# Half of an up product moved from the end of the scan stage to the front of the kernel

## The chip, the core and the metric

The kernel runs on one core of a Trainium2 chip. The metric is the device time of one execution in microseconds. A core has TensorE for matrix products (results go to PSUM, eight banks of 2 KB per partition), VectorE, ScalarE and GpSimd for work on tiles of 128 partitions in SBUF, and SyncE, whose queue issues most of the transfers here. The profile calls them PE (PEld for its weight loads), DVE, ACT, POOL and SP (SPq). Each engine takes its instructions in the order of its own list.

## What is computed

One step of a small encoder with 1024 prompt rows, 32 sample rows and two layers, of width 1024. Layer 0 has a scan mixer (SSD), layer 1 attention. After each mixer a gated product of a second input p is added:

```python
def ple(h, p, up_w, norm_w, gate_w):
    g = jax.nn.sigmoid((rmsnorm(h, norm_w) @ gate_w).astype(F32)).astype(h.dtype)
    return (p @ up_w).astype(h.dtype) * g
...
        hn_p = rmsnorm(hp, ln_w[i])
...
        hp = hp + yp
        hp = hp + ple(hp, p_prompt[i], ple_up_w[i], ple_norm_w[i], ple_gate_w[i])
```

The product `p @ up_w` (256 x 1024 weights) needs neither the mixer nor h: it can be computed at any time before layer 0's gate.

## The kernel before

All products are made of three matmuls on operands that are split into a high and a low part (`wh`, `wl` of a weight; `hh`, `hl` of an activation): high x high, high x low, low x high. `load_weight` issues the load of a weight on SP's queue, makes the high part on ScalarE (or on VectorE, where `eng_h` says so) and the low part, a subtraction, on GpSimd. `gemm` issues the three matmuls for each block of 128 rows.

The scan stage, `phase_ssd`, holds columns of x in three tiles (384, 384 and 292 columns). At its start ten matmuls on a tile of ones (`busy`) run while x arrives. For each tile x is loaded in four quarters; ScalarE, VectorE and GpSimd square it (`sq`), VectorE adds pairs, TensorE sums them over the partitions (`psn`, four matmuls), ScalarE makes `r`, the factor of the norm, with Ln and Exp, VectorE multiplies (`hf`), ScalarE rounds (`hh`) and GpSimd, or VectorE for blocks 1 and 5, subtracts (`hl`). The first products, a 32-column one for dt and block 0 of the input projection, follow on TensorE. Then eight groups of heads are projected, convolved and scanned.

The up product of layer 0, `up_product`, is a generator. Up to its first `yield` it loads the two halves of p transposed (`upr`) and splits them (`upx`). Then, for each of eight output blocks m, 18 matmuls fill three PSUM tiles (`mm`, 352 columns each), ScalarE evacuates them into `upe`, and the block is stored to DRAM (`u_d`). With `nb=4` one weight load and split serves four blocks. In the kernel before all of it, 144 matmuls, stands at the end of the scan stage: the last group's gate and norm (`gate`, `finish`) are written between its loads and its matmuls, so that both run side by side. `finish` walks y in three pieces: squares on ScalarE (`ysq`), a sum on GpSimd, high part on ScalarE (`ysh`), low part on GpSimd (`ysl`), two matmuls that sum over partitions (`psy`), a copy on ScalarE (`yr`); then Ln and Exp of the whole, and VectorE writes y, which is stored. The output projection, `phase_out`, reads y back (`yraw`, split into `yhl`) and multiplies it by `outW` into `pso`: for three output blocks first the 8 older blocks of y, 144 matmuls, then the rest.

The order of the instructions on each engine is set when the kernel is built, by a scheduler with a timeline of its own; a code line that moves can so move instructions of other lines. Pools set limits: `mm` has three PSUM buffers, weights have two buffers of each part, `cx` and `raw`, in which the up product's tiles lie, six each.

Of the kernel before, what the change touches and what calls it, by code (L numbers as in the profile page):

```python
# [10 lines left out]
F32 = mybir.dt.float32  # L11
F32R = mybir.dt.float32r
# [5 lines left out]
P = 128  # L18

T1 = 1060  # L20
RAWB = 6
# [3 lines left out]
T = 1056  # L25
# [147 lines left out]
def bc_last(ap, n):  # L173
    return ap.unsqueeze(len(ap.shape)).to_broadcast(list(ap.shape) + [n])
# [6 lines left out]
def rsqrt(nc, c, out, ps, scale, eps):  # L181
    nc.scalar.activation(out, ps, AF.Ln, bias=eps, scale=scale)
    nc.scalar.activation(out, out, AF.Exp, scale=-0.5)
# [8 lines left out]
def load_weight(c, src, nk, m, scale=None, eng_h=None, wp=None):  # L192
    nc = c.nc
    wp = wp or c.wp
    raw = wp.tile([P, nk, m], F32, tag="wraw", name="wraw")
    nc.sync.dma_start(raw, src)
    if scale is not None:
        nc.gpsimd.tensor_tensor(raw, raw, bc_last(scale, m), op=ALU.mult)
    wh = wp.tile([P, nk, m], F32R, tag="wh", name="wh", bufs=c.whb)
    wl = wp.tile([P, nk, m], F32R, tag="wl", name="wl", bufs=c.whb)  # L200
    if eng_h:
        eng_h.tensor_copy(wh, raw)
    else:
        nc.scalar.activation(wh, raw, AF.Copy)  # L204
    nc.gpsimd.tensor_tensor(wl, raw, wh.bitcast(F32), op=ALU.subtract)  # L205
    return wh, wl


def gemm(c, ps, w, acts, sl, m=P, first=True, last=True):
    wh, wl = w  # L210
    n = len(acts)
    for k, (ah, al) in enumerate(acts):
        a, b = ah[:, sl], al[:, sl]
        for i, (ww, aa) in enumerate(((wh, a), (wh, b), (wl, a))):
            c.nc.tensor.matmul(ps, ww[:, k, :m], aa, start=first and k == 0 and i == 0, stop=last and k == n - 1 and i == 2)  # L215


def split(c, h, l, x, eng_h=None, eng_l=None):
    nc = c.nc
    (eng_h or (lambda o, i: nc.scalar.activation(o, i, AF.Copy)))(h, x)  # L220
    (eng_l or nc.vector).tensor_tensor(l, x, h.bitcast(F32), op=ALU.subtract)  # L221


def pvc(c, name, i=0, n=1, rows=P):
    o, _ = PV[name]
    return c.pv[:rows, o + i : o + i + n]


def up_product(c, i, piece, raw, tiles, ps_tile, evac, nb=1):

    nc, I = c.nc, c.I
    o, n = piece
    acts = []
    for k in range(2):
        x = raw()[:, :n]
        nc.sync.dma_start(x, I[f"pT{i}"][:, k, o : o + n])
        h, l = tiles()[:, :n], tiles()[:, :n]
        split(c, h, l, x)
        acts.append((h, l))
    yield  # L240
    na = -(-n // 512)
    w_ = n // na
    for m in range(8):
        b = m % nb
        if b == 0:
            ws = load_weight(c, I[f"upW{i}"][m // 4][:, 2 * (m % 4) : 2 * (m % 4 + nb)], 2 * nb, P)
        w = [x[:, 2 * b : 2 * b + 2] for x in ws]
        u = evac()
        for a in range(na):
            ps = ps_tile()  # L250
            gemm(c, ps[:, :w_], w, acts, slice(w_ * a, w_ * a + w_))
            nc.scalar.activation(u[:, w_ * a : w_ * a + w_], ps[:, :w_], AF.Copy)  # L252
        c.store(c.u_d[i][m][:, o : o + n], u[:, :n])
        yield
# [8 lines left out]
def phase_ssd(c, ctx):  # L263
    nc, tc, I, O = c.nc, c.tc, c.I, c.O
# [3 lines left out]
    mm = es.enter_context(tc.tile_pool(name="ps_mm", bufs=3, space=bass.MemoryType.PSUM))  # L268
# [8 lines left out]
    kp = es.enter_context(tc.tile_pool(name="keep", bufs=1))  # L277
    with tc.tile_pool(name="xin", bufs=2, side="right") as xp:
        def busy(x, k):

            ps = pc.tile([P, 512], F32, tag="trx", name="busy")
            for _ in range(k):
                nc.tensor.matmul(ps[:, : x.shape[-1]], c.ones, x, start=True, stop=True)

        busy(c.ones, 10)
        for j, (o, n) in enumerate(TILES1):
            xt = xp.tile([P, 8, n], F32, tag=f"xt{j}", name=f"xt{j}", bufs=1)
            for q in range(4):
                nc.sync.dma_start(xt[:, 2 * q : 2 * q + 2, :], I["xT"][:, 2 * q : 2 * q + 2, o : o + n])
            if j == 0:  # L290
                c.load_constants()
                early = [load_weight(c, I["dtW"], 8, 32, eng_h=nc.vector), load_weight(c, I["inW"][0], 8, P, eng_h=nc.vector)]
            ps = pc.tile([P, 512], F32, tag="st", name=f"psn{j}")
            for q in range(4):
                sq = [xp.tile([P, n], F32, tag="sq", name=f"sq{j}_{q}", bufs=6) for _ in range(2)]
                nc.scalar.activation(sq[0], xt[:, 2 * q], AF.Square)
                if j and q % 2:
                    nc.gpsimd.tensor_tensor(sq[1], xt[:, 2 * q + 1], xt[:, 2 * q + 1], op=ALU.mult)
                elif j == 0:
                    nc.vector.tensor_tensor(sq[1], xt[:, 2 * q + 1], xt[:, 2 * q + 1], op=ALU.mult)  # L300
                else:
                    nc.scalar.activation(sq[1], xt[:, 2 * q + 1], AF.Square)
                nc.vector.tensor_tensor(sq[0], sq[0], sq[1], op=ALU.add)
                nc.tensor.matmul(ps[:, :n], c.ones, sq[0], start=q == 0, stop=q == 3)
            r = xp.tile([P, n], F32, tag="r", name=f"r{j}")
            rsqrt(nc, c, r, ps[:, :n], 1.0 / 1024, c.eps)
            if j == 0:
                busy(r, 2)
            for k in range(8):
                hf = xp.tile([P, n], F32, tag="hf", name=f"hf{j}_{k}", bufs=3)  # L310
                nc.vector.scalar_tensor_tensor(hf, xt[:, k], pvc(c, "lnw0", k), r, op0=ALU.mult, op1=ALU.mult)
                hh, hl = hn[j][0][k], hn[j][1][k]
                nc.scalar.activation(hh, hf, AF.Copy)
                (nc.vector if k % 4 == 1 else nc.gpsimd).tensor_tensor(hl, hf, hh.bitcast(F32), op=ALU.subtract)

    def mblock(*blocks, ws=None):

        ws = ws or [load_weight(c, wsrc, 8, m) for wsrc, m, _ in blocks]
        for j, (o, n) in enumerate(TILES1):
            for w, (_, m, evac) in zip(ws, blocks):  # L320
                ps = mm.tile([P, 512], F32, tag="mm", name="mm")
                acts = list(zip(hn[j][0], hn[j][1]))
                gemm(c, ps[:m, :n], w, acts, slice(0, n), m)
                evac(j, o, n, ps[:m, :n])
# [92 lines left out]
    def gate(g, b, S):  # L417

        z = raw_block(I["inW"][6 * g + 4 + b])[:, 3:]
        th = kp.tile([P, 3 + T1], F32, tag="raw", name="zs", bufs=RAWB)[:, 3:]  # L420
        sigmoid2(nc, z, th, z)
        yb = S["y"][:, b]
        nc.gpsimd.tensor_tensor(yb, yb, z, op=ALU.mult)
# [120 lines left out]
    def bc_blocks(g):  # L544
        Ss[g]["B"] = conv_block(I["inW"][6 * g], 16 + g, None if g else first)
        Ss[g]["C"] = conv_block(I["inW"][6 * g + 1], 24 + g)

    def x_block(g, b):
        Ss[g].setdefault("x", []).append(conv_block(I["inW"][6 * g + 2 + b], 2 * g + b))
# [5 lines left out]
    for g in range(G):  # L555
        scan_group(g, Ss[g])
        if g + 1 < G:
            bc_blocks(g + 1)
        if g:
            gate(g - 1, 0, Ss[g - 1])  # L560
            gate(g - 1, 1, Ss[g - 1])
        if g + 1 < G:
            x_block(g + 1, 0)
        else:
            gate(g, 0, Ss[g])
        if g:
            finish(g - 1, Ss[g - 1])
        if g + 1 < G:
            x_block(g + 1, 1)
        else:  # L570
            up = up_product(c, 0, (0, T), lambda: kp.tile([P, T1], F32, tag="cx", name="upr", bufs=6),
                            lambda: kp.tile([P, 3 + T1], F32R, tag="raw", name="upx", bufs=RAWB),
                            lambda: mm.tile([P, 512], F32, tag="mm", name="mm"),
                            lambda: kp.tile([P, T1], F32, tag="cx", name="upe", bufs=6), 4)
            next(up)
            gate(g, 1, Ss[g])
            finish(g, Ss[g])
# [546 lines left out]
def run(*gens):  # L1124
    for g in gens:
        for _ in g:
            pass
# [177 lines left out]
def build(tc, nc, I, O, dbg=None, ngroups=8, upto=9):  # L1305
# [4 lines left out]
    with ctx:  # L1310
# [40 lines left out]

        ln_exp()
        phase_ssd(c, ctx)
        if upto < 2:
            return
# [130 lines left out]
```

## Time and profile before

| | us |
|---|---|
| median of 3 runs (2016.47 to 2018.35) | 2016.96 |
| the profiled execution | 2012.76 |
| its span, first to last instruction | 2011.0 |
| TensorE busy | 1932.2 |
| VectorE busy | 1282.6 |
| ScalarE busy | 1023.8 |
| GpSimd busy | 971.6 |

The span is what the profile's rows cover; the execution's time holds 1.8 us around it. The profiled execution is a run of its own, beside the three that were timed. Starts are counted from the first instruction. A row with an idle time in brackets names who ended the wait.

### The profile page before, as it was taken

How to read it: one execution, taken by the hardware profiler on the slowest of the kernel's cores; microseconds unless marked ns; L12 is line 12 of the kernel's file. 1: busy time of each engine (PE TensorE's matmuls, PEld its weight loads, DVE VectorE, ACT ScalarE, POOL GpSimd, SP SyncE). 2: the span in 40 equal slices, each digit the busy share in tenths (PEclk: the TensorE clock that was granted, in tenths of full speed). 3: DMA queues.
4: the chain of work that ended last, by engine and by line, in shares of the span. 5: the costliest groups of instructions: out<-in, count | busy, mean ns of one | idle time of the engine just before them, and what ended most of it. 6: DMA issues, size and time to landing. Idle time of an engine off the chain costs nothing. (4 is left out here: it accounts for less than half of the span.)

```text
span 2011.0 us, 32658 instructions
## 1 busy us (share of the span) xinstructions
PE 1932.2 (96%) x12871; PEld 1773.9 (88%) x12871; DVE 1282.6 (64%) x1601; ACT 1023.8 (51%) x1757; POOL 971.6 (48%) x813
## 2 busy tenths in 40 slices
PE   7989999999999999999998999999899999999999
PEld 5989899999999998999998999777777777779999
DVE  7898575858576675443267534274688787986544
ACT  4444444453545457334243432587687877754331
POOL 5433334344444444454678443122545453645772
PEclk8999999999999999999999999999999999999999
DMA  3143333334242446544333312533512221315432
GB/s 130 53 94 90 85 91 77 86 99 99 73 104 64 104 109 214 178 140 161 100 114 119 94 55 85 164 105 96 118 47 72 54 66 36 108 59 193 127 126 74
DMA packets 110730, 204.27 MB, mean 102 GB/s; under 512 B 18224, under 2 KB 60720, under 8 KB 110448
## 3 DMA queue, kind: packets, MB, share of 16 engines
q1 hardware_dynamic: 105472, 193.17, 32.5%
q0 software_dynamic: 2800, 6.91, 1.9%
q8 instruction: 101, 1.65, 0.3%
q10 hardware_dynamic: 2304, 2.10, 0.3%
q14 instruction: 53, 0.43, 0.1%
HBM read 156.81 MB, written 38.83 MB: 97 GB/s over the span
## 5 line engine op out<-in xcount | busy, mean ns | idle before, releaser
L205 POOL TENSOR_TENSOR wl<-wraw,wh 128x1024 fp32r<-128x1024 f32 (+2 forms) x185 | 374.1, 2024 | 413.7 <-ACT wh L204 371.5
L215 PE MATMUL mm<-hh,wh 128*128 128x384 f32 (+3 forms) x1176 | 386.0, 329 | 4.7 <-ACT raw L330 4.5
L215 PE MATMUL mm<-hl,wh 128*128 128x384 f32 (+3 forms) x1176 | 387.6, 330 | 0.0
L215 PE MATMUL mm<-hh,wl 128*128 128x384 f32 (+3 forms) x1176 | 385.4, 328 | 0.0
L204 ACT ACTIVATE wh<-wraw 128x1024 fp32r<-128x1024 f32 (+3 forms) x183 | 159.1, 869 | 280.8 <-PE pso L215 117.8
L215 PE MATMUL pso<-yhl,wh 128*128 128x264 f32 x1536 | 283.5, 285 | 5.6 <-ACT upe L252 2.9
L215 PEld LDWEIGHTS pso<-yhl,wh 128*128 128x128 f32 x1536 | 239.8, 189 | 7.0 <-DVE yhl L221 3.8
L215 PEld LDWEIGHTS mm<-hh,wh 128*128 128x128 f32 (+1 forms) x1176 | 220.3, 187 | 8.9 <-ACT raw L330 5.2
L215 PEld LDWEIGHTS mm<-hl,wh 128*128 128x128 f32 (+1 forms) x1176 | 220.8, 188 | 4.6 <-issue 2.4
L215 PEld LDWEIGHTS mm<-hh,wl 128*128 128x128 f32 (+1 forms) x1176 | 220.5, 187 | 4.2 <-issue 1.9
L215 PE MATMUL pso<-yhl,wl 128*128 128x264 f32 x768 | 219.3, 286 | 4.1 <-POOL wl L205 4.1
L413 DVE SCALAR_TENSOR_TENSOR cx<-raw,pv,cx 128x1060 f32<-128x1060 f32 x96 | 132.6, 1381 | 88.3 <-ACT cx L411 87.6
L215 PE MATMUL psi<-yhl,wh 128*128 128x264 f32 (+1 forms) x896 | 167.0, 287 | 3.9 <-ACT yhl L220 3.8
L215 PEld LDWEIGHTS pso<-yhl,wl 128*128 128x128 f32 x768 | 145.2, 189 | 4.7 <-POOL wl L205 4.7
L488 POOL TENSOR_TENSOR hm<-hT,cd_all 128x256 f32<-128x256 f32 x64 | 67.6, 1057 | 165.5 <-DVE hT L490 100.7
L215 PE MATMUL pg<-hH,wl 128*128 128x264 f32 x512 | 145.9, 285 | 0.7 <-POOL wl L205 0.7
L215 PE MATMUL pg<-hH,wh 128*128 128x264 f32 x512 | 145.9, 285 | 0.0
L215 PE MATMUL pg<-hL,wh 128*128 128x264 f32 x512 | 145.7, 285 | 0.0
L215 PEld LDWEIGHTS psi<-yhl,wh 128*128 128x128 f32 (+1 forms) x896 | 138.2, 185 | 5.6 <-ACT yhl L220 4.0
L1238 PE MATMUL st<-qk 128*128 128x512 f32 (+2 forms) x576 | 139.8, 358 | 0.9 <-ACT pf L1244 0.5
L215 PE MATMUL psi<-yhl,wl 128*128 128x264 f32 (+1 forms) x448 | 129.6, 289 | 1.1 <-POOL wl L205 1.1
L1259 POOL TENSOR_TENSOR pl<-pf,ph 128x512 fp32r<-128x512 f32 x64 | 81.3, 1271 | 102.1 <-DVE ph L1258 93.5
(517 smaller groups left out, 4579.0 us busy)
## 6 DMA issues: line engine op xcount, KB each, us to landing
wraw<-in_inW SPq DMA_DIRECT2D x48, 512.0 KB, 3.5
ex<-acs_d SPq DMA_DIRECT2D x32, 512.0 KB, 5.2
wraw<-in_outW SPq DMA_DIRECT2D x32, 512.0 KB, 3.6
yraw<-y_d SPq DMA_DIRECT2D x32, 264.0 KB, 4.6
u<-u_d SPq DMA_DIRECT2D x32, 264.0 KB, 2.8
eb<-ea_d SPq DMA_DIRECT2D x64, 128.0 KB, 4.0
y_d<-y SPq DMA_DIRECT2D x16, 512.0 KB, 2.9
wraw<-in_gateW SPq DMA_DIRECT2D x16, 512.0 KB, 3.6
```

The lines of the kernel that those rows point to most:

```text
L204: nc.scalar.activation(wh, raw, AF.Copy)
L205: nc.gpsimd.tensor_tensor(wl, raw, wh.bitcast(F32), op=ALU.subtract)
L215: c.nc.tensor.matmul(ps, ww[:, k, :m], aa, start=first and k == 0 and i == 0, stop=last and k == n - 1 and i == 2)
L413: nc.vector.scalar_tensor_tensor(xh, raw[:, k : k + T1], pvc(c, "cw", 4 * b + k), xh, op0=ALU.mult, op1=ALU.add)
L488: nc.gpsimd.tensor_tensor(hm.rearrange("p (h q) -> p h q", q=64), hT.rearrange("p (h q) -> p h q", q=64), bc_last(cd_all[:, hs, ch], 64), ...
L1238: nc.tensor.matmul(ps[:, :n], a_[:, ks], b_[:, q], start=t == 0, stop=t == 2)
L1259: (nc.gpsimd if idx in L_POOL else nc.vector).tensor_tensor(pl[:, :n], pf[:, :n], ph[:, :n].bitcast(F32), op=ALU.subtract)
```

## The change

`up_product` can now do a part of the blocks (`ms`) with a weight that is handed in. Blocks 0 to 3 are done at the front of the scan stage: their weight and p are loaded and split ahead of x (`next(up)`), the weight's high part on VectorE, and the matmuls are written behind the norm of x's first tile (`run(up)`). The loads and splits of the first projection weights (`early`) move from ahead of that norm to behind it. Blocks 4 to 7 stay at the end of the stage, and p is loaded and split there a second time.

```diff
-def up_product(c, i, piece, raw, tiles, ps_tile, evac, nb=1):
+def up_product(c, i, piece, raw, tiles, ps_tile, evac, nb=1, ms=range(8), weights=None):
...
-    for m in range(8):
+    for m in ms:
         b = m % nb
         if b == 0:
-            ws = load_weight(c, I[f"upW{i}"][m // 4][:, 2 * (m % 4) : 2 * (m % 4 + nb)], 2 * nb, P)
+            ws = weights or load_weight(c, I[f"upW{i}"][m // 4][:, 2 * (m % 4) : 2 * (m % 4 + nb)], 2 * nb, P)
...
+        def up0(ms, **kw):
+            return up_product(c, 0, (0, T), lambda: kp.tile([P, T1], F32, tag="cx", name="upr", bufs=6),
+                              lambda: kp.tile([P, 3 + T1], F32R, tag="raw", name="upx", bufs=RAWB),
+                              lambda: mm.tile([P, 512], F32, tag="mm", name="mm"),
+                              lambda: kp.tile([P, T1], F32, tag="cx", name="upe", bufs=6), 4, ms, **kw)
+
         busy(c.ones, 10)
+
+        up = up0(range(4), weights=load_weight(c, I["upW0"][0], 8, P, eng_h=nc.vector))
+        next(up)
         for j, (o, n) in enumerate(TILES1):
...
             if j == 0:
                 c.load_constants()
-                early = [load_weight(c, I["dtW"], 8, 32, eng_h=nc.vector), load_weight(c, I["inW"][0], 8, P, eng_h=nc.vector)]
...
+            if j == 0:
+                early = [load_weight(c, I["dtW"], 8, 32, eng_h=nc.vector), load_weight(c, I["inW"][0], 8, P, eng_h=nc.vector)]
+                run(up)
...
-            up = up_product(c, 0, (0, T), lambda: kp.tile([P, T1], F32, tag="cx", name="upr", bufs=6),
-                            lambda: kp.tile([P, 3 + T1], F32R, tag="raw", name="upx", bufs=RAWB),
-                            lambda: mm.tile([P, 512], F32, tag="mm", name="mm"),
-                            lambda: kp.tile([P, T1], F32, tag="cx", name="upe", bufs=6), 4)
+            up = up0(range(4, 8))
             next(up)
```

How this moves instructions is seen at three places. TensorE at the front, before: the sums of the first tile follow the ten matmuls on ones, and the first projection (`mm` from `hh`) follows `r`.

```order
L283 MATMUL busy_186<-ones_115 128x128 x10
L304 MATMUL psn0_219<-sq0_0_220,ones_115 128x384
L304 MATMUL psn0_219<-sq0_1_226,ones_115 128x384
L304 MATMUL psn0_219<-sq0_2_232,ones_115 128x384
L304 MATMUL psn0_219<-sq0_3_238,ones_115 128x384
L283 MATMUL busy_247<-r0_244,ones_115 128x384 x2
L215 MATMUL mm_424<-hh0_0_132,wh_209 32x384
```

In the changed kernel, from the third to the last of these sums (`upx` 205 and 206 are high and low part of p's first half, 211 and 212 of its second):

```order
L312 MATMUL psn0_225<-sq0_2_238,ones_115 128x384
L215 MATMUL mm_353<-upx_205,wh_199 128x352
L215 MATMUL mm_353<-upx_206,wh_199 128x352
L215 MATMUL mm_353<-upx_205,wl_200 128x352
L215 MATMUL mm_353<-upx_211,wh_199 128x352
L215 MATMUL mm_353<-upx_212,wh_199 128x352
L215 MATMUL mm_353<-upx_211,wl_200 128x352
L312 MATMUL psn0_225<-sq0_3_244,ones_115 128x384
```

Ahead of these rows stand 36 up matmuls, with the first two sums among them: 42 of the 72 stand ahead of the first tile's last sum, 18 more ahead of the second tile's sums, and the last 12 ahead of the first projection.

ScalarE at the same place, before, from Ln and Exp of `r` to the first two rounded blocks:

```order
L182 ACTIVATE r0_244<-psn0_219,eps_120 128x384
L183 ACTIVATE r0_244<-r0_244 128x384
L296 ACTIVATE sq1_0_288<-xt1_282 128x384
L302 ACTIVATE sq1_0_289<-xt1_282 128x384
L313 ACTIVATE hh0_0_132<-hf0_0_250 128x384
L313 ACTIVATE hh0_1_134<-hf0_1_254 128x384
```

In the changed kernel:

```order
L182 ACTIVATE r0_250<-psn0_225,eps_120 128x384
L304 ACTIVATE sq1_2_422<-xt1_404 128x384
L310 ACTIVATE sq1_2_423<-xt1_404 128x384
L183 ACTIVATE r0_250<-r0_250 128x384
L252 ACTIVATE upe_352<-mm_361 128x352
L304 ACTIVATE sq1_3_428<-xt1_404 128x384
L252 ACTIVATE upe_352<-mm_369 128x352
L304 ACTIVATE sq2_0_475<-xt2_469 128x292
L321 ACTIVATE hh0_0_132<-hf0_0_256 128x384
L252 ACTIVATE upe_378<-mm_379 128x352
L321 ACTIVATE hh0_1_134<-hf0_1_260 128x384
```

Two squares of the second tile now stand between Ln and Exp, and evacuations of the up product and more squares ahead of `hh`. On VectorE 36 rows stand from the first `hf` to the last where there were 38: three sums of the second tile's squares stand ahead of them now, and the cast of block 0's weight among them.

TensorE at the end of the scan stage, before, from the low part of the last norm piece (`psy` with `ysl`) on; two more tiles of the up product stand between it and the output projection (`pso`):

```order
L260 MATMUL psy_7528<-ysl_7525,ones_r_117 128x292
L215 MATMUL mm_7743<-upx_7399,wh_7652 128x352
L215 MATMUL mm_7743<-upx_7400,wh_7652 128x352
L215 MATMUL mm_7743<-upx_7399,wl_7653 128x352
L215 MATMUL mm_7743<-upx_7405,wh_7652 128x352
L215 MATMUL mm_7743<-upx_7406,wh_7652 128x352
L215 MATMUL mm_7743<-upx_7405,wl_7653 128x352
```

In the changed kernel, from the end of the last up tile on:

```order
L215 MATMUL mm_7763<-upx_7527,wl_7665 128x352
L260 MATMUL psy_7628<-ysl_7625,ones_r_117 128x384
L259 MATMUL psy_7639<-ysh_7635,ones_r_117 128x384
L260 MATMUL psy_7639<-ysl_7636,ones_r_117 128x384
L259 MATMUL psy_7650<-ysh_7646,ones_r_117 128x292
L260 MATMUL psy_7650<-ysl_7647,ones_r_117 128x292
L215 MATMUL pso_7893<-yhl_7798,wh_7898 128x264
```

The last two norm pieces, which lay among up matmuls, now follow one another directly, and the output projection stands right behind them.

## Rows read from the trace of the kernel before

**Rows 1.** The page: TensorE's busy time, its share of the span and its matmuls.

```profile
PE 1932.2 (96%) x12871; PEld 1773.9 (88%) x12871; DVE 1282.6 (64%) x1601; ACT 1023.8 (51%) x1757; POOL 971.6 (48%) x813
```

**Rows 2.** Busy time by stretches: the stretch, its length, each engine's busy time and instructions, TensorE's granted clock, the DMA engines' share and GB/s.

```profile
5.00:10.00 5.00, 3.98 (x12) 1.49 (x10) 3.79 (x10) 1.86 (x4) 0.72 (x1) 1.00 1.06 382
...
20.00:25.00 5.00, 5.00 (x15) 3.48 (x15) 5.00 (x8) 2.17 (x5) 2.46 (x3) 0.50 0.00 0
...
785.00:790.00 5.00, 4.84 (x29) 4.70 (x30) 5.00 (x5) 5.00 (x13) 3.08 (x2) 1.00 0.80 311
```

**Rows 3.** Timeline of the first norm, 0 to 50 us: start, duration, engine, line, operation; in brackets the idle time ahead and who ended it. L304 is psn, L182 and L183 are Ln and Exp, L311 is hf.

```profile
4.05 0.56 DVE L300 TENSOR_TENSOR sq<-xt 128x384 f32<-128x384 f32 x1 [2.78 <-DMA xt<-in_xT]
...
7.45 0.55 DVE L300 TENSOR_TENSOR sq<-xt 128x384 f32<-128x384 f32 x1
...
8.76 0.91 PE L304 MATMUL psn<-sq,ones 128*128 128x384 f32 x2 [0.25 <-DVE sq L303]
...
9.71 0.58 ACT L182 ACTIVATE r<-psn,eps 128x384 f32<-128x384 f32 x1 [1.80 <-PE psn L304]
...
10.21 0.69 DVE L202 CAST wh<-wraw 128x1024 fp32r<-128x1024 f32 x1 [1.01 <-DMA wraw<-in_inW]
10.32 0.52 ACT L183 ACTIVATE r<-r 128x384 f32<-128x384 f32 x1
10.88 4.34 DVE L311 SCALAR_TENSOR_TENSOR hf<-xt,pv,r 128x384 f32<-128x384 f32 x3
...
11.26 0.52 ACT L296 ACTIVATE sq<-xt 128x384 f32<-128x384 f32 x1 [0.42 <-DMA xt<-in_xT]
...
15.15 1.35 DVE L303 TENSOR_TENSOR sq<-sq,sq 128x384 f32<-128x384 f32 x1
...
18.34 2.45 DVE L303 TENSOR_TENSOR sq<-sq,sq 128x384 f32<-128x384 f32 x2
...
26.56 0.84 DVE L303 TENSOR_TENSOR sq<-sq,sq 128x292 f32<-128x292 f32 x2 [1.04 <-ACT sq L302]
28.96 2.92 DVE L311 SCALAR_TENSOR_TENSOR hf<-xt,pv,r 128x384 f32<-128x384 f32 x3 [1.57 <-ACT r L183]
...
45.80 0.51 DVE L311 SCALAR_TENSOR_TENSOR hf<-xt,pv,r 128x292 f32<-128x292 f32 x1
```

**Rows 4.** Timeline of TensorE in the same stretch: a matmul in 20 to 25 us, the end of the second tile and the start of the third.

```profile
22.30 0.52 PE L215 MATMUL mm<-hh,wl 128*32 128x384 f32 x1
22.62 0.52 PE L215 MATMUL mm<-hh,wh 128*32 128x384 f32 x1
...
42.62 0.34 PE L215 MATMUL mm<-hh,wl 128*128 128x384 f32 x1
47.22 0.45 PE L215 MATMUL mm<-hh,wh 128*32 128x292 f32 x1 [4.26 <-ACT raw L330]
...
53.01 0.29 PE L215 MATMUL mm<-hh,wh 128*128 128x292 f32 x1
53.14 0.30 PE L215 MATMUL mm<-hl,wh 128*128 128x292 f32 x1
```

**Rows 5.** The up product at the end of the scan stage: timeline of its splits and of three matmuls, and the answer on the tile upe (least, median and longest duration in ns, first and last start).

```profile
765.38 1.09 ACT L220 ACTIVATE upx<-upr 128x1056 fp32r<-128x1056 f32 x1
...
770.15 1.24 DVE L221 TENSOR_TENSOR upx<-upr,upx 128x1056 fp32r<-128x1056 f32 x1
...
783.22 0.49 PE L215 MATMUL mm<-upx,wh 128*128 128x352 f32 x2
783.54 0.33 PE L215 MATMUL mm<-upx,wl 128*128 128x352 f32 x1
...
L252 ACT ACTIVATE upe<-mm x24: 443/462/534, 776.3 to 805.6; 128x352 f32<-128x352 f32 x24
```

**Rows 6.** Timeline from the first up matmul to the output projection, 774 to 812 us. L527 is ysq, L221 ysl, L534 the copy yr, L182 and L183 Ln and Exp with the table loads ahead of them.

```profile
774.68 0.32 PE L215 MATMUL mm<-upx,wh 128*128 128x352 f32 x1
...
781.17 0.59 PE L215 MATMUL mm<-upx,wh 128*128 128x352 f32 x2 [2.12 <-ACT upe L252]
...
794.76 1.02 POOL L221 TENSOR_TENSOR ysl<-ysq,ysh 128x384 fp32r<-128x384 f32 x1
...
796.42 0.69 ACT L527 ACTIVATE ysq<-y 128x584 f32<-128x584 f32 x1
...
798.57 0.82 POOL L221 TENSOR_TENSOR ysl<-ysq,ysh 128x292 fp32r<-128x292 f32 x1 [0.56 <-ACT ysh L220]
...
801.47 0.41 ACT L534 ACTIVATE yr<-psy 128x292 f32<-128x292 f32 x1
801.89 1.28 ACT L182 ACT_TABLE_LOAD   x1
803.19 1.18 ACT L182 ACTIVATE yr<-yr,eps 128x1060 f32<-128x1060 f32 x1
...
806.07 0.51 PE L215 MATMUL pso<-yhl,wh 128*128 128x264 f32 x2 [2.93 <-ACT upe L252]
...
807.33 1.09 ACT L183 ACTIVATE yr<-yr 128x1060 f32<-128x1060 f32 x1
...
811.35 0.41 PE L215 MATMUL pso<-yhl,wh 128*128 128x264 f32 x2
...
811.72 0.41 PE L215 MATMUL pso<-yhl,wh 128*128 128x264 f32 x2
```

## Prediction

> **What bounds the kernel now.** I read the page's shares of busy time first: TensorE is busy 96% of the span [rows 1], so a microsecond is won only where TensorE waits or runs slowly. I then went to the two places that the change touches. At the **front** the table by stretches shows a core that fills its DMA engines, at 382 GB/s, and a TensorE at clock 0.50 in 20 to 25 us [rows 2]. The timeline of the first norm names the chain: quarters of x land, VectorE squares and adds, TensorE sums four psn matmuls, ScalarE makes r, and from 10.88 us VectorE works through the products hf until 46.31 us [rows 3]. TensorE follows it: it has nothing after 42.62 us, waits 4.26 us for an evacuation that stands behind the last hh on ScalarE, and starts the third tile at 47.22 us with 24 matmuls that take 5.8 us to 53.01, 0.24 us each, where the next one takes 0.13 [rows 4]. So the front ends when VectorE's last hf is done; TensorE has room there. At the **seam** between the scan and the output projection, TensorE runs the 144 up matmuls at 0.163 us each (three in 0.49) [rows 5], while ScalarE, busy all of 785 to 790 us [rows 2], and GpSimd walk the last group's norm (ysq, ysh, ysl, three times) beside 24 evacuations. The last evacuation stands behind a table load, and the first pso matmul waits 2.93 us for it, until 806.07 us [rows 6].
>
> **The seam, part by part.** *Taken away:* 72 matmuls, 72 x 0.163 = 11.7 us of TensorE; 12 evacuations of 0.46 us [rows 5], 5.5 us of ScalarE; four stores and one weight load. The operand pT is still loaded and split there, so that cost stays. *What comes last instead:* up to the twelfth evacuation both orders read alike, so the up matmuls that are left end near 790.6 us. Behind them TensorE's queue now holds the psy pairs of the second and third piece, and only then pso: pso can't go before the norm has given its third piece. That chain moves little. GpSimd's second ysl ends at 795.78 us as before, since the weight split ahead of it stays; then the third ysq starts 0.6 us sooner, at 795.8 instead of 796.42, no longer behind two evacuations. From there to the end of the third ysl took 2.97 us [rows 6], so it is done at 798.8, and two psy matmuls later, at 799.2 us, pso begins: **6.9 us sooner**, not 11.7. *What that costs:* TensorE waits about 8.4 us there instead of 2.93. After the 2.93 us, the first ten triples of pso took 5.28 us, to 811.35, where the next triple takes 0.37 [rows 6]: 1.6 us lost. In 20 to 25 us the engine was busy throughout and stayed low all five [rows 2], so a longer wait may lose 2.5 us: **0.9 us back**. *What could be late next:* the last two blocks of y. Behind the third psy stand an evacuation, two table loads, Ln and Exp, 0.41 + 1.28 + 1.18 + 1.28 + 1.09 = 5.2 us, so Exp ends at 804.4 instead of 808.42 [rows 6], 4.0 us sooner; VectorE's y and their stores follow. They are needed only after 144 pso matmuls and most of the next 48, some 20 us behind the first; I put 0.1 us. The seam gives **-5.9 us**; bounds -2.9 (only the wait for the evacuation goes) and -11.7 (all the matmuls' time).
>
> **The front, part by part.** *Transfers:* 512 KB of weights and 2 x 528 KB of pT now stand first on SP's queue, ahead of x: 1.61 MB, 4.2 us at 382 GB/s [rows 2]. So x lands from 8.2 to 11.7 us instead of 4.05 to 7.45 [rows 3]. *Splits:* two of 1.09 us on ScalarE, two of 1.24 on VectorE [rows 5] and a weight split on GpSimd. pT lands at about 5.8 and 7.2 us and the splits lie in the wait for x, but for the second low part, which stands behind x's first square on VectorE and ends near 10.4 us. *Matmuls:* the last psn matmul now stands behind 42 up matmuls. The first 18 need that low part and end near 11.5; the other 24 take 3.9 us and the four psn between them, 0.91 us each when alone [rows 3] and about half of that in a stream, some 1.8. That makes 17.2 us, where it was 9.67. Then r: Ln 0.58, two squares of x's second tile that now stand between (1.04), Exp 0.52 [rows 3] and two hops, 19.6. **VectorE's first hf starts 8.7 us later**. *What VectorE saves behind it:* three sums of the second tile's squares now stand ahead of hf, 1.35 + 2.45 = 3.8 us; block 0's weight cast, 0.69 at 10.21 us [rows 3], stands behind it now: -3.1. Its two waits of 1.04 and 1.57 us [rows 3] came from the second tile's squares and their psn, which are now done ahead: -2.6. *New:* on ScalarE five evacuations stand among the hh; the first three, with two squares, hold hh 1, for which VectorE's hl 1 waits some 1.5 us, the others 0.5: +2.0. Sum 8.7 - 3.1 - 2.6 + 2.0 = **+5.0 us** on the end of the norm and on the third tile's start. Bounds: +0.5 (only the transfers delay, 4.2 + 2.0 - 5.7) and +10.7 (no saving on VectorE comes); I take the middle, since each term has its own row. The stores of u wait at SP behind all of x, with 0 GB/s in 20 to 25 us [rows 2]: nothing. GpSimd's subtract for the second weight now falls among the hl pieces, as it fell among the hf before: nothing, up to 2.4 us at worst, in the bound. TensorE has 16 instead of 9 matmuls to do after the last hl piece of the second tile, which shortens its 4.26 us wait to about 3.1; behind 2.93 us at 806 us matmuls ran slowly too [rows 6], so I leave the 24 x 0.11 = 2.6 us of slow matmuls in [rows 4]; as a bound they go.
>
> In 20 to 25 us TensorE ran its real work at 0.50, the 1.2 GHz level [rows 2]; the up matmuls will keep it busy ahead of that work. The Trainium skill (TensorE: Matmul & The Clock Gate, "What's actually happening") says that low is the resting state and that work lifts it. By that rule alone the five slow microseconds would give back 2.5 us more and the sum would be 3.4 us below the median; by the rows they give nothing beyond VectorE's two waits, since TensorE still stood idle for 4.26 us at the end of the front [rows 4].
>
> **Between the two** the orders read alike; further on a few rows of the attention part trade places, which I price at nothing, within 0.5 us.
>
> **Sum.** +5.0 - 5.9 = -0.9 us. The profiled execution took 2012.76 us, 1.76 more than its span, and lies 4.2 us below the median of the runs, 2016.96; its terms carry over as differences: 2016.96 - 0.9 = **2016.0 us**. A measurement of this kernel can tell about 0.2%, 4.0 us, from no change; this is inside it.
>
> **Rivals.** (1) *The front hides nearly all of it, faster.* If the 42 matmuls start as soon as the first pT is split, at 7.2 us, they end with their psn near 14.3 instead of 17.2, when x has just landed: -2.9; and if the clock stays up behind TensorE's shorter wait, the 2.6 us of slow matmuls go too. -0.9 - 5.5 = -6.4: 2010.6. For it: behind a wait of 2.12 us at 781 us three matmuls soon took 0.49 again [rows 5, 6]; against it, the second low part behind x's first square. (2) *The clock falls ahead of the up matmuls, slower.* The ten warming matmuls end near 5.5 us and the operands come between 7 and 10.4. If the clock falls in that wait, the 42 matmuls in front of the norm run at 0.32 us, as one of 384 columns did at 22.30 [rows 4], instead of 0.163: 42 x 0.157 = 6.6 us on a chain that everything follows, 2022.6. It turns the sign from 6 slow matmuls on (0.9 / 0.157) and passes 0.2% from 31. Against it: the clock stood at 1.00 in 5 to 10 us with work in bits [rows 2]. (3) *The seam gives no more than its old wait.* If the norm's last piece comes when it came before, pso starts little sooner and with a colder clock: -2.9 instead of -5.9, 2019.1. For it, the norm's chain is almost unchanged; against it, the twelve evacuations that leave ScalarE.
>
> **How the numbers follow.** Forecast 0.40, (1) 0.30, (2) 0.19, (3) 0.11. The predicted time is the forecast's, 2016.0. The forecast's own range, with half of each bound, is 2012 to 2020. The range of 8 in 10 goes to just beyond (1) and to (2): 2009.5 to 2022.5. Faster by over 0.2%: nearly all of (1) and a little of the forecast, 0.32. Slower by over 0.2%: (2) and a little of the others, 0.22. Within: 0.46.
>
> **What would show it.** In the changed kernel: the first hf on VectorE near 19.6 us, the last near 51, and the third tile's start on TensorE near 52 (right for the front); under 49 speaks for (1), over 56 for (2), with a granted clock under 1 between 10 and 20 us. At the seam, counted from the first up matmul there: first psy of the last pair 24 us on and pso 24.5 us on instead of 31.4, with a granted clock near 0.5 behind it. Wrong would be: a pso that waits for yhl or for weights after 144 matmuls, or a move of the time that neither place holds.

## The result and the profile after

The changed kernel takes 2021.07 us (median of 20 executions, 2015.63 to 2025.97) beside 2015.74 us for the kernel before (20 executions, 2009.43 to 2019.67). The ratio is 1.0029 with a 95% interval of 1.0019 to 1.0039: it is slower, by 3.8 to 7.9 us. The forecast was 0.9 us faster. The time lies in the range, but the forecast had the sign wrong.

The profiled execution took 2022.79 us with a span of 2021.0; the one of before took 2012.76 with 2011.0. These two differ by 10 us, more than the medians do, so single traces are compared below place by place, and each place is held against the other traces of the study.

**The front.** First the table by stretches (as [rows 2], with the stretch behind the seam added): length, each engine's busy time, TensorE's granted clock, DMA share, GB/s.

```profile
5.00:10.00 5.00, 3.13 (x11) 2.38 (x10) 3.29 (x4) 3.14 (x4) 2.39 (x2) 1.00 1.04 385
20.00:25.00 5.00, 5.00 (x26) 4.07 (x25) 2.80 (x6) 4.82 (x14) 1.74 (x2) 1.00 1.05 410
...
785.00:790.00 5.00, 3.38 (x22) 3.10 (x20) 1.62 (x1) 4.97 (x8) 3.51 (x2) 1.00 0.88 268
...
805.00:810.00 5.00, 2.96 (x9) 2.24 (x10) 1.27 (x2) 2.63 (x5) 1.93 (x3) 0.50 0.98 379
```

Then the timeline of the changed kernel from the warm-up to the first transpose of the scan (answers to [rows 3, 4]; L312 is psn, L182 and L183 are Ln and Exp, L319 is hf):

```profile
1.06 4.64 PE L283 MATMUL busy<-ones 128*128 128x128 f32 x20 [1.06 <-DVE eps L1355]
6.94 1.25 PE L215 MATMUL mm<-upx,wh 128*128 128x352 f32 x3 [1.25 <-ACT upx L220]
8.81 0.66 PE L215 MATMUL mm<-upx,wh 128*128 128x352 f32 x1 [0.62 <-DVE upx L221]
9.27 0.49 PE L215 MATMUL mm<-upx,wl 128*128 128x352 f32 x1
9.56 0.49 PE L215 MATMUL mm<-upx,wh 128*128 128x352 f32 x1
...
13.37 1.12 PE L312 MATMUL psn<-sq,ones 128*128 128x384 f32 x2
...
14.65 0.32 PE L215 MATMUL mm<-upx,wl 128*128 128x352 f32 x1
14.81 0.48 PE L215 MATMUL mm<-upx,wh 128*128 128x352 f32 x2
...
19.48 0.81 PE L312 MATMUL psn<-sq,ones 128*128 128x384 f32 x2
...
20.33 0.58 ACT L182 ACTIVATE r<-psn,eps 128x384 f32<-128x384 f32 x1 [0.18 <-PE psn L312]
...
22.24 1.67 DVE L319 SCALAR_TENSOR_TENSOR hf<-xt,pv,r 128x384 f32<-128x384 f32 x3
...
54.02 0.51 DVE L319 SCALAR_TENSOR_TENSOR hf<-xt,pv,r 128x292 f32<-128x292 f32 x1
...
55.44 0.45 PE L215 MATMUL mm<-hh,wh 128*32 128x292 f32 x1 [3.78 <-ACT raw L341]
...
108.11 0.30 PE L461 MATMUL trx<-cst,cx 128*128 128x128 f32 x1 [1.98 <-DVE cx L189]
```

Look at the starts, not at the durations. From 9.27 to 9.56 us one up matmul of 352 columns takes 0.29 us, and all 18 ahead of the first psn go at that pace; from 14.65 to 14.81 one takes 0.16. Per column 0.29 us is the pace of the 384 columns at 22.30 us of before, where the granted clock stood at 0.50 [rows 2, 4]: the 1.2 GHz level. The column of the granted clock reads 1.00 in 5 to 10 us and doesn't show it. The warm-up's rows do: its 20 passes (two to a matmul) take 4.64 us, 0.23 each, where eight more of them in e4 below take 1.29, 0.16 each. In this trace the level had not risen by the time the up matmuls came. The last psn ends at 20.29 us (17.2 forecast, 9.67 before), the first hf starts at 22.24 (19.6; 10.88), the last hf ends at 54.53 (51.3; 46.31), and the third tile starts at 55.44 (52; 47.22 [rows 3, 4]). The first transpose of the scan stands at 108.11; before it stood at 101.13.

**The seam**, from the first up matmul there to the output projection (as [rows 6]):

```profile
784.08 0.32 PE L215 MATMUL mm<-upx,wh 128*128 128x352 f32 x1
...
790.58 0.59 PE L215 MATMUL mm<-upx,wh 128*128 128x352 f32 x2 [2.19 <-ACT upe L252]
...
802.79 0.69 PE L259 MATMUL psy<-ysh,ones_r 128*128 128x384 f32 x1 [2.65 <-ACT ysh L220]
805.14 0.69 PE L260 MATMUL psy<-ysl,ones_r 128*128 128x384 f32 x1 [1.65 <-POOL ysl L221]
807.46 0.61 PE L259 MATMUL psy<-ysh,ones_r 128*128 128x292 f32 x1 [1.63 <-ACT ysh L220]
808.34 0.61 PE L260 MATMUL psy<-ysl,ones_r 128*128 128x292 f32 x1 [0.27 <-POOL ysl L221]
808.74 0.64 PE L215 MATMUL pso<-yhl,wh 128*128 128x264 f32 x2
```

Here the forecast holds. From the first up matmul to pso are 24.66 us (24.5 forecast, 31.39 before [rows 6]); the psy pairs now wait four times, 6.2 us in all, for the norm of the last group, and the clock is 0.50 in 805 to 810 us, where the last pair and the first pso matmuls stand.

**Far behind both**, in the second output product at 1820 to 1850 us, VectorE's queue has another order. The timeline of VectorE there, first of the kernel before (L221 yhl: subtractions for the coming half; L664 hf: evacuation of pso):

```profile
1824.77 1.38 DVE L221 TENSOR_TENSOR yhl<-yraw,yhl 128x528 fp32r<-128x528 f32 x2 [7.72 <-ACT yhl L220]
1827.52 2.08 DVE L221 TENSOR_TENSOR yhl<-yraw,yhl 128x528 fp32r<-128x528 f32 x3 [1.37 <-ACT yhl L220]
1829.63 0.71 DVE L664 TENSOR_TENSOR hf<-pso,xres 128x528 f32<-128x528 f32 x1
```

and then of the changed kernel, where L672 is hf, with the matmul that waits for it:

```profile
1833.57 3.38 DVE L221 TENSOR_TENSOR yhl<-yraw,yhl 128x528 fp32r<-128x528 f32 x5 [8.36 <-ACT yhl L220]
1838.16 0.71 DVE L221 TENSOR_TENSOR yhl<-yraw,yhl 128x528 fp32r<-128x528 f32 x1 [1.21 <-ACT yhl L220]
1840.28 1.42 DVE L221 TENSOR_TENSOR yhl<-yraw,yhl 128x528 fp32r<-128x528 f32 x2 [1.41 <-ACT yhl L220]
1841.73 1.32 DVE L672 TENSOR_TENSOR hf<-pso,xres 128x528 f32<-128x528 f32 x2
...
1842.58 0.48 PE L215 MATMUL pso<-yhl,wh 128*128 128x264 f32 x2 [0.77 <-DVE hf L672]
```

Before, the first evacuation stood behind five subtractions; now it stands behind eight, and TensorE waits for it. From the first pso matmul there to the first pg matmul are 97.5 us; before they were 96.0.

### The profile page after: what moved, and what is told of

It is laid out like the page before. It is cut to its first block, busy times and chain, and to the rows that moved or that the text cites. A ratio compares the mean times of both kernels' runs of the same rounds, so it can differ in the third digit from the quotient of the medians.

```text
span 2021.0 us, 32673 instructions
## 1 busy us (share of the span) xinstructions
PE 1936.9 (96%) x12871; PEld 1776.7 (88%) x12871; DVE 1295.0 (64%) x1604; ACT 1024.7 (51%) x1758; POOL 967.6 (48%) x813
## 5 line engine op out<-in xcount | busy, mean ns | idle before, releaser
L204 ACT ACTIVATE wh<-wraw 128x1024 fp32r<-128x1024 f32 (+2 forms) x182 | 157.8, 868 | 271.1 <-PE pso L215 110.5
```

## The experiments

**Theory 1**: the front costs what its trace shows and the seam gives what its trace shows. **Theory 2** (rival): the front's cost is the transfers alone. **Theory 3** (rival): the loss arises elsewhere, through the other order of the work behind the seam.

**e1, the front alone** (against the changed kernel):

```diff
-            up = up0(range(4, 8))
+            up = up0(range(8))
```

> The front of the changed kernel with the seam of the kernel before: blocks 0 to 3 are made at the front and all eight blocks again at the end of the scan stage, so four blocks are made twice. Theory 1 (the whole loss is the norm's delay at the front, 7.0 us in the two traces at 60 us, and the seam gives its 6.7 us back): 7 us over the kernel before, pso 31 us behind the first up matmul of the seam. Theory 2 (the transfers ahead of x are what delays the norm): the same here. Theory 3 (front and seam cancel at +0.3, and some 5 us more are lost behind the seam, through the other order of the work in the attention part and behind it): 12 us over before if that comes with the front, 7 if it comes with the shorter seam.

Measured 2025.89 us beside 2014.76, ratio 1.0056 (1.0039 to 1.0072): 7.9 to 14.5 us over, middle 11.3. The first transpose comes at 108.56, pso 31.6 us behind the first up matmul. Its table by stretches shows the slow up matmuls in the granted clock, as the changed kernel's does not:

```profile
10.00:15.00 5.00, 5.00 (x17) 4.39 (x17) 2.84 (x7) 2.33 (x5) 0.00 (x0) 0.53 1.08 375
```

More than the front's 7 us is lost, so theory 1 alone falls short; the 12 us of theory 3 lie in the interval.

**e2, the seam alone.** Blocks 0 to 3 are left out; the results of blocks 4 to 7 are stored twice.

```diff
+        if i == 0:
+            c.store(c.u_d[i][m - 4][:, o : o + n], u[:, :n])
...
-        up = up0(range(4), weights=load_weight(c, I["upW0"][0], 8, P, eng_h=nc.vector))
-        next(up)
...
                 c.load_constants()
+                early = [load_weight(c, I["dtW"], 8, 32, eng_h=nc.vector), load_weight(c, I["inW"][0], 8, P, eng_h=nc.vector)]
...
-            if j == 0:
-                early = [load_weight(c, I["dtW"], 8, 32, eng_h=nc.vector), load_weight(c, I["inW"][0], 8, P, eng_h=nc.vector)]
-                run(up)
```

> The seam of the changed kernel with the front of the kernel before: blocks 0 to 3 of the up product are left out, and the results of blocks 4 to 7 are stored a second time in their place. Theories 1 and 2: the seam gives its 6.7 us (31.4 less 24.7 from the first up matmul to pso), so 6 to 7 us under before. Theory 3: the loss behind the seam eats most of it, 0 to 2 us under before, and the trace shows the stretch from pso to the end some 5 to 7 us longer than before's 1204.9 us.

Measured 2011.66 us beside 2014.76, ratio 0.9985 (0.9970 to 0.9999): 0.2 to 6.0 us under, middle 3.0. Its trace has the whole gain (24.55 us from the first up matmul, 774.62, to pso):

```profile
797.88 0.61 PE L261 MATMUL psy<-ysh,ones_r 128*128 128x292 f32 x1 [1.39 <-ACT ysh L220]
798.76 0.61 PE L262 MATMUL psy<-ysl,ones_r 128*128 128x292 f32 x1 [0.27 <-POOL ysl L221]
799.17 0.64 PE L215 MATMUL pso<-yhl,wh 128*128 128x264 f32 x2
```

but its second output product takes 97.2 us. Timed, the gain lies between the 6 to 7 us of theories 1 and 2 and the 0 to 2 of theory 3. The sign that theory 3 named is not there: from pso to the end this trace takes 1204.6 us, where before took 1204.9. e1 and e2 together (+11.3 - 3.0 = +8.3) agree with the change within their intervals.

**e3, transfers and splits alone:**

```diff
-                run(up)
...
-            up = up0(range(4, 8))
+            up = up0(range(8))
```

> The transfers and the splits of the up product's operands stand at the front as in the changed kernel, but no up matmul does; all eight blocks are made at the end, with loads of their own, so the front's operands are not used. Theory 1 (the up matmuls ahead of the norm's sums make the delay, the transfers only part of it): first hf at 16 to 18 us instead of 10.9 and 22.2, 2 to 4 us over before. Theory 2 (the transfers alone do it): first hf at 20 to 22 us, 7 us over before. Theory 3 says nothing of the front; 5 us more than either if its loss comes with the splits and loads.

Measured 2020.76 us beside 2014.76, ratio 1.0027 (1.0014 to 1.0040). The trace:

```profile
10.84 5.55 PE L312 MATMUL psn<-sq,ones 128*128 128x384 f32 x8 [5.15 <-DVE sq L311]
...
17.59 5.08 DVE L319 SCALAR_TENSOR_TENSOR hf<-xt,pv,r 128x384 f32<-128x384 f32 x3 [0.20 <-ACT r L183]
...
50.67 0.45 PE L215 MATMUL mm<-hh,wh 128*32 128x292 f32 x1 [3.80 <-ACT raw L340]
```

The first hf is 6.7 us late, as theory 1 had it (17.59, short of theory 2's 20 to 22), the third tile only 3.5, and the first transpose (103.30) 2.2. Theory 2 falls: transfers and splits together make less than half of the delay of the third tile, which is 8.2 us in the changed kernel. The measured 2.8 to 8.1 us are again more than the front shows.

**e5, the loads behind the first tile's x** (the two lines that make `up` move into `if j == 0`, behind `c.load_constants()`):

> The changed kernel with the loads of upW and pT put behind the x of the first norm tile and the constants; on TensorE the first tile's four sums then stand ahead of all up matmuls, and most of these ahead of the second tile's sums. Theory 1: the first hf comes at 11 to 12 us as before, the up matmuls run while VectorE makes the first tile, a part of the 7.0 us stays (1 to 4 us, by the evacuations among the casts of ScalarE and the later x tiles), the seam keeps its 6.7: 3 to 6 us under the kernel before. Theory 2: the same or a little less, as x of tiles 1 and 2 still waits for 1.6 MB (4.2 us at 382 GB/s): 1 to 3 us under before. Theory 3: 5 us more than these, 0 to 2 us over before.

Measured 2023.94 us beside 2014.76, ratio 1.0052 (1.0032 to 1.0072). This fell for every theory: the first hf does come at 11.40 us, but the third tile starts at 58.57.

```profile
14.93 2.05 DVE L221 TENSOR_TENSOR upx<-upr,upx 128x1056 fp32r<-128x1056 f32 x1
...
20.49 2.05 DVE L221 TENSOR_TENSOR upx<-upr,upx 128x1056 fp32r<-128x1056 f32 x1
...
22.59 0.66 PE L215 MATMUL mm<-upx,wh 128*128 128x352 f32 x1 [2.55 <-DVE upx L221]
...
31.59 0.57 ACT L182 ACTIVATE r<-psn,eps 128x384 f32<-128x384 f32 x1
...
39.10 0.36 PE L215 MATMUL mm<-hh,wh 128*32 128x384 f32 x1 [0.59 <-ACT upe L252]
```

The two splits now stand among the products hf, at 2.05 us instead of 1.24 [rows 5]; the evacuations stand among ScalarE's casts, and the second tile's r comes at 31.59. The last hf ends at 52.22, 5.9 us later than before. That is only half of the third tile's 11.4 us; the rest stands in TensorE's own list. All 72 up matmuls stand there ahead of the first projection. They wait for their operands, and it starts at 39.10, where before it started at 12.66:

```profile
12.66 0.54 PE L215 MATMUL mm<-hh,wh 128*32 128x384 f32 x2 [0.21 <-ACT hh L313]
```

The third tile then follows directly on the projections of the first two, without the wait behind VectorE's last hf that before and the changed kernel have.

**e7, two blocks, behind all of x** (with a weight tile of their own in the norm's pool; `nb` becomes 2, so the weights at the seam are loaded for two blocks at a time too, and the loads and splits of `early` stand ahead of the norm again):

```diff
+            if j == 2:
+                ur, uh, ul = (xp.tile([P, 4, P], d, tag=t, name=t, bufs=1) for t, d in (("ur", F32), ("uh", F32R), ("ul", F32R)))
...
+                up = up0(range(2), weights=(uh, ul))
+                next(up)
...
+            if j == 2:
+                run(up)
...
-            up = up0(range(4, 8))
+            up = up0(range(2, 8))
```

> Two blocks instead of four move to the front, with their loads behind the x of all three norm tiles and with a weight tile of their own, so that none of the norm's transfers or sums stands behind them; the 36 up matmuls stand ahead of the first product of the scan's inputs instead. Theory 1: the first hf as in before (10.9 us), the third tile's products 1 to 3 us later, the seam 3 to 5 us shorter: 1 to 4 us under before, less what the other order behind the seam takes. Theory 2: the same. Theory 3: that order takes 2 to 5 us, so within 2 us of before.

Measured 2020.76 us beside 2015.03, ratio 1.0026 (1.0013 to 1.0039). The seam gives 3.6 us (27.75 from the first up matmul to pso), but the third tile starts at 55.74, the first transpose at 107.08. The splits on VectorE (2.32 and 1.24 us) stand among hf once more, but the last hf ends at 49.24, only 2.9 us later than before, where the third tile is 8.5 later. As in e5 the first projection stands behind the up matmuls:

```profile
39.07 0.36 PE L215 MATMUL mm<-hh,wh 128*32 128x384 f32 x1
```

From there to the third tile TensorE is busy all of 16.6 us. The time, 2.6 to 7.9 us over before, fell for all three theories.

**e6a and e6b, the order alone.** The kernel before, with one line behind `finish(g, Ss[g])`; e6a has 3 where e6b has 4:

```diff
+            busy(c.ones, 4)
```

> The kernel before with three idle-filling matmuls of 128x128 (about 0.2 us each) written behind the end of the scan stage, where TensorE waits for others anyway; the order of the work behind the seam stays word for word that of the kernel before. All theories: within 1 us of the kernel before.

> The same with four such matmuls instead of three. The scheduler then writes the attention part and the second output product in another order: three of VectorE's subtractions and two of ScalarE's casts for the second half now stand ahead of the first evacuation of pso, and the loads of u stand three in a row ahead of xres, as in the changed kernel, in the seam alone and in every kernel of the first batch. Theory 3, as it now stands (that other order is a cost of its own, and any edit of this size may bring it): 2 to 5 us over its sister with three matmuls, and in the trace the second output product 1 to 2 us longer than the 96.0 us of before. Theory 1 (front and seam are all there is): within 1 us of its sister.

Measured beside 2015.03: e6a 2014.59, ratio 0.9997 (0.9985 to 1.0009); e6b 2017.22, ratio 1.0012 (1.0001 to 1.0022). One idle matmul more, and 2.6 us between the medians, uncertain by 2 to 3; the second output product takes 95.4 us in e6a and 96.6 in e6b. Theory 3 holds in part: the order costs something, less than the whole loss. (The attention part is written in another order too, but takes no longer in e6b's trace.)

**e4, 14 warm-up matmuls** in the changed kernel:

```diff
-        busy(c.ones, 10)
+        busy(c.ones, 14)
```

> The changed kernel with 14 instead of 10 warm-up matmuls, which fill the gap of 1.2 us ahead of the first up matmul. If that gap is what leaves the first up matmuls at the low level (0.293 us each instead of 0.163), they run at the high level from the start, the last sum of the first tile ends 2 to 3 us sooner, and the kernel comes 2 us under the changed one (2 to 4 us over before). If the level does not hang on it: last sum and time as in the changed kernel, or up to 0.6 us later.

Measured 2016.05 us beside 2015.03, ratio 1.0011 (0.9997 to 1.0025). The timeline of its front:

```profile
1.06 5.93 PE L283 MATMUL busy<-ones 128*128 128x128 f32 x28 [1.06 <-DVE eps L1355]
6.88 0.76 PE L215 MATMUL mm<-upx,wh 128*128 128x352 f32 x3
8.72 0.43 PE L215 MATMUL mm<-upx,wh 128*128 128x352 f32 x1 [1.08 <-DVE upx L221]
8.98 0.32 PE L215 MATMUL mm<-upx,wl 128*128 128x352 f32 x1
9.14 0.32 PE L215 MATMUL mm<-upx,wh 128*128 128x352 f32 x1
...
17.21 0.81 PE L312 MATMUL psn<-sq,ones 128*128 128x384 f32 x2
...
19.97 1.67 DVE L319 SCALAR_TENSOR_TENSOR hf<-xt,pv,r 128x384 f32<-128x384 f32 x3
...
53.18 0.32 PE L215 MATMUL mm<-hh,wh 128*32 128x292 f32 x1 [3.78 <-ACT raw L341]
```

With no gap ahead of 6.88 us every up matmul goes at 0.16 (8.98 to 9.14); the last psn starts at 17.21 instead of 19.48, the first hf at 19.97, the third tile at 53.18. That is the forecast's front within 1.2 us, at the level that the forecast took. The four matmuls close the gap and lengthen the work ahead of it at once, and no run separates the two; a wait of 1.08 us ahead of 8.72 stayed and slowed nothing. By the ratios e4 lies some 3.6 us under the changed kernel, uncertain by 3.

**e8, the order mended**, in the changed kernel; **e9**, the same with 14 warm-up matmuls:

```diff
+            if hf and nkb == 8 and k == 0:
+                for _ in range(1):
+                    nc.sync.dma_start(raw[:, :8], src_d[k][:, o : o + 8])
```

> The changed kernel with one small load more (8 columns of yraw, loaded again at once with the whole) ahead of the second half of the second output product. It does no work; it moves the scheduler's clock, so that the first evacuation of pso there stands ahead of the last subtractions of the second half again, nearly as in the kernel before; the attention part keeps the changed kernel's order. If the order there costs what the traces show (96.0 us from pso to pg before, 97.5 in the changed kernel): that stretch back at about 96, and 1 to 2 us under the changed kernel timed beside it. If the loss sits elsewhere: the same time as the changed kernel.

> The same small load, and 14 warm-up matmuls instead of 10, which took the up matmuls to the high level and the third tile 2.3 us forward. Both parts add up: 1 us under the kernel with 14 alone (2016.05, with the kernel before at 2015.03), so level with the kernel before, within 2 us either way.

**e10**, the kernel before with 14, and **e11**, the changed kernel unaltered:

> The kernel before with 14 warm-up matmuls and nothing else; the order of all other work is kept. It is the control for the gain of 14 in the changed kernel. If the clock matters only where up matmuls run early: level with the kernel before, within 1 us (the last warm-up ends at 7.5 us, so the first sums of the norm may start up to 2 us later, with the first hf then up to 1 us later). If the clock helps the norm's own sums as well (0.91 us for two at the low level): 1 to 2 us under the kernel before.

> The changed kernel once more, timed beside these and with a second profile: 4 to 8 us over the kernel before. What its two traces share is the change; what they don't is the spread from one execution to the next: front at 60 us +7 and pso 24.7 us behind the first up matmul in both, the second output product at 97 to 98 us.

Measured beside 2015.56: e8 2019.05, ratio 1.0011 (0.9997 to 1.0025); e9 2016.54, ratio 1.0009 (0.9994 to 1.0024); e10 2014.35, ratio 0.9994 (0.9981 to 1.0007); e11 2021.11, ratio 1.0030 (1.0016 to 1.0044). In e8 the first evacuation stands behind five subtractions again, and TensorE no longer waits for hf:

```profile
1831.98 0.71 DVE L221 TENSOR_TENSOR yhl<-yraw,yhl 128x528 fp32r<-128x528 f32 x1 [8.01 <-ACT yhl L220]
1835.90 2.57 DVE L221 TENSOR_TENSOR yhl<-yraw,yhl 128x528 fp32r<-128x528 f32 x4 [3.21 <-ACT yhl L220]
1838.50 0.71 DVE L675 TENSOR_TENSOR hf<-pso,xres 128x528 f32<-128x528 f32 x1
```

The product takes 96.2 us there, and e8 lies 2.1 us under e11 beside it by the medians, 3.8 by the ratios; 1 to 2 were expected. e9 lies level with e4's distance from before, and its product takes 96.5 us as in e4; mending adds nothing that can be told there. Fourteen warm-up matmuls bring no change clear of the noise in the kernel before (e10), so the gain in e4 belongs to the changed front. No version that computes the whole is clear of the noise below the kernel before.

## Why the prediction was wrong

The stages as all fourteen traces of the study have them, by means of the kernels that share the stage (us; the spread in brackets):

| stage | as before | as changed | difference | forecast |
|---|---|---|---|---|
| front, to the first transpose | 100.7 (99.2 to 101.5, five) | 108.3 (108.1 to 108.6, four) | +7.6 | +5.0 |
| the same with 14 warm-up matmuls | 100.7 | 106.2 (106.1 and 106.3) | +5.5 | +5.0 |
| first up matmul of the seam to pso | 31.4 (30.9 to 31.7, six) | 24.8 (24.6 to 25.1, seven) | -6.5 | -6.9 |
| the first 64 triples of pso | 24.2 (23.0 to 25.7, six) | 25.3 (24.4 to 26.1, seven) | +1.1 | +0.9 |
| second output product | 95.6 (95.4 to 96.0, three) | 97.1 (96.5 to 98.5, nine) | +1.5 | 0 |

(e7, with two blocks, is left out of the rows on the seam; e8 and e9, with the mended order, of the last row: 96.2 and 96.5. e5's 98.5 there has a granted clock of 0.98 where all others have 1.00; without it the mean is 96.9, +1.3.) The sum is +7.6 - 6.5 + 1.1 + 1.5 = +3.7 us; the timed difference is 5.8 (3.8 to 7.9). With 14 warm-up matmuls the sum is +1.6, and the ratios of e4 and e9 say 2.2 and 1.8, each uncertain by 3.

1. **The seam was right**, in mechanism and size: -5.4 where the forecast had -5.9. The psy pairs hold pso, the clock is low behind them, and no pso waits for yhl at its start. Rival (3), which left the seam -2.9, is out.
2. **The failed step is "The first 18 need that low part and end near 11.5; the other 24 take 3.9 us".** It took 0.163 us for each up matmul. In the four traces with this front and 10 warm-up matmuls, 10 to 18 of these 18 ran at 0.29, and the last psn ended at 19.3 to 20.6 instead of 17.2. In the trace shown it is all 18, 18 x 0.13 = 2.3 us, and e4's third tile starts 2.3 us sooner (53.18 for 55.44); over the four traces and the two with 14, the first transpose comes 2.1 us sooner. In the three others the first three to five were still at the high level, and it fell behind them; there the column of the granted clock shows it, 0.79, 0.53 and 0.74 in 10 to 15 us in e11, e1 and e8. The sign that the prediction named, a granted clock under 1 between 10 and 20 us, is there in these three and not in the trace shown. This is rival (2) in part: the forecast priced it as all 42 at the low level or none, and set "the clock stood at 1.00 in 5 to 10 us" against it, by a column that shows 1.00 in the changed kernel's trace as well, where the pace says otherwise. Its own turning point, 6 slow matmuls, was passed: this term alone turns the sign. A smaller part of the same step holds at the high level too: from the first psn to the end of the last took 6.6 us in e4 (11.43 to 18.02), where 3.9 + 1.8 = 5.7 were forecast.
3. **The second failed step is "further on a few rows of the attention part trade places, which I price at nothing, within 0.5 us".** The orders show the swap without any run; the prediction didn't ask who waits for the evacuation that moved back, and named the attention part, where the swaps cost nothing that can be seen, but not the output product behind it. It is 1.3 to 1.5 us in the traces; the timed pairs say 2.6 (e6b over e6a), 2.1 (e11 over e8) and nothing (e9 beside e4), each uncertain by 2 to 3. TensorE's waits in that stretch add up to 0.9 to 1.4 us in the three traces with the old order, 1.7 to 2.6 in the nine with the new and 1.4 to 1.5 in the two mended. The wait for hf is 0 to 0.8 us of it; a wait of some 1.3 us for GpSimd's part of a weight is another, which the old order has in two of its three traces, at 0.5 and 1.4. The traces tell the two orders apart; that the place of the evacuation is all of it they do not show.
4. **The rest of the front was right in mechanism.** VectorE is the chain, the transfers are only part of the delay, and from first to last hf it saves 3.1 us (32.3 where it took 35.4 [rows 3]; 3.7 forecast). The trace of before is an early one here: in the other four with its front hf takes 33.2 to 34.6 us, so that the saving is 2.0 against the mean of the five, and its first hf starts 1.2 us before the mean of the five. At the high level the front costs 5.5, and its bounds hold. Rival (1) did not come: the 42 matmuls ended with their psn at 18.0 even at the high level, not at 14.3. e5 and e7 do not show that the room on TensorE can't be used: there the first projection stood behind the up matmuls, and an order that keeps it ahead of them was not run.
5. **What stays open:** about 2 us between the sum of the places and the timed difference. The scan took 670 to 676 us and the attention part 538 to 544 in these traces, with spreads of 3 to 6 us among kernels of the same order too, so a single trace can't place them. With 14 warm-up matmuls sum and times agree within 0.6 us, so a part of these 2 us may come with the slow front; that they belong to the change at all is not shown.

The Trainium skill (TensorE: Matmul & The Clock Gate, "What's actually happening") calls the low level the resting state, which work lifts. The traces agree at this place: with 10 warm-up matmuls and a gap of 1.1 to 1.7 us behind them most of the first 18 up matmuls were slow, with 14 and no gap none was. The 2.5 us that the rule alone would have added as a gain did not appear: the clock stood at 1.00 in 20 to 25 us, and VectorE, not TensorE, was what the front waited for.

## What to carry to other kernels

Price a matmul that is moved to the start of a kernel at the level that the pace there shows, not at a clock column alone, and look at the warm-up and the gap between it and the first real work; four warm-up matmuls more took 2.1 us off the front here. Free time on one engine can be used only by work whose operands are ready: in e5 and e7 the moved matmuls waited for splits on VectorE, and the first projection waited behind them. And when a scheduler sets the order, read every swap that an edit brings, however far away, for who waits behind it: one idle matmul more went with 1.2 us at a place 1000 us behind it.

## What the runs showed that was not expected

The spread between executions goes with the mean granted clock. Of 23 executions of the kernel before beside e1, e2, e3 and e5, the one at 0.993 took 2010.97 us and the one at 0.983 took 2020.07; over all kernels a time is about 1 us longer for each 0.001 of clock less, and in these 23 the two are correlated at -0.8. Which is the cause is not shown, since the clock is also low behind TensorE's waits. Nor does it explain every pair: the two profiles compared above lie 10 us apart, at 0.989 for the faster and 0.991 for the slower. A stage is better compared over several traces.
